# GpSimd's preparation products of a two-block layer kernel, queued behind the last gating product

## The chip, the core and the metric

The kernel runs on one core of a Trainium2 chip. The core has TensorE (PE, the matrix engine), VectorE (DVE), ScalarE (ACT), GpSimd (POOL) and SyncE (SP, which here only issues weight DMAs). Each engine works through its own queue in order, and an instruction that must wait for another engine holds up all behind it on its own engine. The metric is the time of one execution on the device, in microseconds (us).

## The reference, cut

Two layers follow each other on 256 tokens of width 1024. The stretch of interest is the feed-forward part at the end of the first layer, and what the second layer needs before it can start.

```python
def conv_glu_ffn(h, w_up, conv_w, w_down):          # D_FF = 2816 = 22 blocks of 128
    up = causal_dwconv(h @ w_up, conv_w)            # three taps along the positions
    gate, val = jnp.split(up, 2, axis=-1)
    return (jax.nn.silu(gate) * val) @ w_down

def s5_branch(u, a_re, a_im, log_dt, b_re, b_im, c_re, c_im, d, w_glu, b_glu):
    lam = lax.complex(a_re, a_im)
    a_bar = jnp.exp(lam * dt)
    b_bar = ((a_bar - 1.0) / lam)[..., None] * lax.complex(b_re, b_im)
    ...                                             # linear recurrence over the positions

def blockdiag(x, w):                                # w: (n_blocks, 4, 4)
    ...
gates = concat([q, k, v]) @ w_if + b_if             # q, k, v come out of blockdiag
```

The second layer's recurrence (`s5_branch`) is computed four positions at a time, so complex powers of `a_bar` times `b` and `c` are needed as matrices. Its gates are computed by folding the 4x4 blocks into `w_if`. Both depend on weights alone, so the kernel computes them while the first layer's feed-forward part runs. This is "the preparation".

## The kernel before, in words

**Weights.** All weight matrices arrive as units of eight 128x128 fp32 tiles (512 KB). For precision each unit is split in two fp32r parts: ScalarE rounds it to `wh` (L339), VectorE computes the remainder `wl` (L340). A product is then three matmuls (L405 to L407 in `mm3`): `wh` with the rounded activation, `wh` with its remainder, `wl` with the rounded activation. Four buffers each for `wh` and `wl` let the split run up to three units ahead of TensorE.

**The feed-forward loop.** `up(i)` for block i of 22 multiplies two units (48 matmuls into `u`), applies the three taps (ScalarE L1888, VectorE L1889 and L1890, for the gate half and the value half), then Silu on ScalarE (L1891), then the gating product of the two halves, L1892: on GpSimd for blocks 0 to 18, on VectorE for 19 to 21. "Product i" below is L1892 of block i. The result is split for the next matmuls: ScalarE rounds it to `ffnr` (L429 in `split`), VectorE computes the remainder (L430). `down(i - 2)` multiplies one unit (24 matmuls into `acc`, L1903 to L1905).

**The preparation.** `_prep` is a generator. Each time TensorE enters a new unit, `tick` lets it run one step, so its instructions are written in between the loop's. GpSimd does most of its work: eight complex products in `paced` (L564), each of four multiplies into the scratch `x1`, `x2` (tile ZZ, printed as s_3381) and two sums; three go to `bx` (tile BX, s_3382), one to `c0` (tile TT, s_3380), four to `cx` (tile CX, s_3379). With them go a small negation to `nc0` (L575) and a large one of 128x2048 elements (L583). Last come eight rounds of three block-diagonal expansions of 128x128 (`expand`, L492), each round followed by three small matmuls into `pf` (L639 to L641). The expansions of a round overwrite those of the round before, so they wait for its `pf`. TensorE also transposes `bx` (`pt`, L591, eight groups of four) and multiplies it by `c0` (`pk`, L599, four groups of 16); ScalarE copies the results out (L592, L602).

**What sets the order.** The tile framework keeps the dependencies and chooses for each engine an order by when it expects each instruction to be ready. So an instruction of `_prep` that depends on little can be put far ahead of its place in the program. `issue_after(ins)` adds, without a semaphore, the condition that what is written inside stands behind `ins` on `ins`'s engine.

Of the kernel before, what the change touches and what calls it, by code (L numbers as in the profile page):

```python
# [14 lines left out]
ALU = mybir.AluOpType  # L15
# [9 lines left out]
NFF = DFF // P  # L25
# [239 lines left out]
class _K:  # L265
    def __init__(self, ctx, tc, I):
        self.tc, self.nc, self.I = tc, tc.nc, I
        self.misc = ctx.enter_context(tc.tile_pool(name="misc", bufs=1))
        self.bigp = ctx.enter_context(tc.tile_pool(name="big", bufs=8))
        self.g8p = ctx.enter_context(tc.tile_pool(name="g8", bufs=3))  # L270
        self.wp = ctx.enter_context(tc.tile_pool(name="w", bufs=4))
        self.dram = ctx.enter_context(tc.tile_pool(name="dram", bufs=1, space=bass.MemoryType.DRAM))
        self.pl = ctx.enter_context(tc.tile_pool(name="pl", bufs=4, space=PSUM))
        self.banks = ctx.enter_context(ExitStack())
        self.pm = self.banks.enter_context(tc.tile_pool(name="pm", bufs=4, space=PSUM))
        self.src = [I["W"][u] for u in range(N_UNITS)] + [I["U"][i] for i in range(NE)] + [I["V"][i] for i in range(NE)]
        self.raw, self.units, self.done = [], {}, 0
        self.at = -1
        self.bg, self.credit, self.rate = [], 0.0, RATE
        self.splits, self.last = [], None  # L280
        self.n = 0

    def name(self, s):
# [64 lines left out]
    def behind(self, lag=0):  # L348

        s = ExitStack()  # L350
        for ins in (*self.splits[-1 - lag], self.last):
            if ins is not None:
                s.enter_context(self.tc.issue_after(ins))
        return s

    def step(self, gen, lag):
        if len(self.splits) <= lag:
# [110 lines left out]
def _prep(K, dump):  # L468

    nc, I, cols = K.nc, K.I, K.cols  # L470
    g = nc.gpsimd
    act, mm, tp = nc.scalar.activation, nc.tensor.matmul, nc.tensor.transpose
    tt, ts, stt = nc.vector.tensor_tensor, nc.vector.tensor_scalar, nc.vector.scalar_tensor_tensor
    EW, CX, TT, ZZ, BX = (K.big(f"s5{i}") for i in range(5))
    ew = EW.a(16, 2, P)
    cx = [CX.a(16, 4, 32) for _ in range(2)]
# [13 lines left out]
    def expand(w, e, dst):  # L490

        g.tensor_tensor(dst.rearrange("p (a b) -> p a b", b=4), _bc(w[:, 4 * e:4 * e + 4], 1, 32), _bc(msk, 2, 4), ALU.mult)  # L492
# [66 lines left out]
    def paced(dr, di, xr_, xi, yr, yi):  # L559

        ops = []
        cmul(dr, di, xr_, xi, yr, yi, x1, x2, lambda *z: ops.append(z))
        for n, z in enumerate(ops):
            g.tensor_tensor(*z)  # L564
            if n not in (0, 3):
                yield 0.1

# [4 lines left out]
    for t in (2, 1, 0):  # L572
        yield from paced(bx[0][:, :, t], bx[1][:, :, t], bx[0][:, :, t + 1], bx[1][:, :, t + 1], bar, bai)
    yield from paced(c0[0], c0[1], C[:, 0], C[:, 1], bc(kr), bc(ki))
    g.tensor_scalar(nc0, c0[1], -1.0, None, ALU.mult)  # L575

    def outputs():
        pr, pi_ = c0
        for t in range(4):
            qr, qi = cx[0][:, :, t], cx[1][:, :, t]  # L580
            yield from paced(qr, qi, pr, pi_, bar, bai)
            pr, pi_ = qr, qi
        g.tensor_scalar(cx[1], cx[1], -1.0, None, ALU.mult)  # L583

    def inputs():

# [45 lines left out]
    nc.vector.tensor_reduce(nqk, pr4.rearrange("p (m d) -> p m d", d=4), AX.X, ALU.add)  # L632

    for e in range(8):
        for i in range(3):
            expand(tr[i], e, ex[:, i])
        yield 0.3
        pf = K.ps("pf")
        mm(pf[:, 0:8], ex[:, 0], wif[:, e], start=True, stop=False)  # L639
        mm(pf[:, 0:8], ex[:, 1], wif[:, 8 + e], start=False, stop=True)  # L640
        mm(pf[:, 8:16], ex[:, 2], wif[:, 16 + e], start=True, stop=True)  # L641
        nc.scalar.copy(fold[:, :, e], pf[:, 0:16].rearrange("p (a b) -> p a b", a=2))
# [691 lines left out]
def trainium_kernel(ctx, tc, I, O, dump=None, stop=None):  # L1334
# [536 lines left out]
    def up(i):  # L1871
        nonlocal rs, nrm, prep
        u, raw = ua[i % 4], i < RAW
        if i == RAW:
            K.finish(nrm)
        ps = [K.ps("u"), K.ps("u")]
        for e in range(2):
            K.lin(f"up{i}", e * 8, 8, h0 if raw else hh, l0 if raw else hl, ps[e][:, :T1])
            if i == 0 and e == 1:
                rs = K.rstd()  # L1880
                nrm = K.start(K.normed(xr, COL["ffn_norm_g"], rs, hi1, lo1, T1))
                prep = K.start(_prep(K, dump))
            for f in (0, 1) if i == 0 and e else (e,) if i else ():
                v, n = ps[f][:, :T1], f * NFF + i
                if raw:
                    tt(uv[:, f], v, rs, ALU.mult)
                    v = uv[:, f]
                act(u[:, f], v, AF.Copy, scale=col("ffn_conv_w", 2 * 44 + n))  # L1888
                stt(u[:, f, 1:], v[:, :T1 - 1], col("ffn_conv_w", 44 + n), u[:, f, 1:], ALU.mult, ALU.add)  # L1889
                stt(u[:, f, 2:], v[:, :T1 - 2], col("ffn_conv_w", n), u[:, f, 2:], ALU.mult, ALU.add)  # L1890
        act(u[:, 0], u[:, 0], AF.Silu)  # L1891
        (nc.gpsimd.tensor_tensor if i < NFF - 3 else tt)(u[:, 0], u[:, 0], u[:, 1], ALU.mult)  # L1892
        if i > 0 and i <= NFF - 3:
            K.split(*uh[(i - 1) % 4], ua[(i - 1) % 4][:, 0])
        if i >= NFF - 3:
            K.split(*uh[i % 4], u[:, 0])
# [77 lines left out]
```

## Time and profile before

| | |
|---|---|
| median of 3 runs | 1595.97 us (1594.9 to 1597.15) |
| the profiled execution | 1592.86 us, of it a span of 1591.0 us |
| busy in the span | PE 1535.2 (96%), DVE 1146.4 (72%), ACT 832.5 (52%), POOL 237.4 us (15%) |
| chain that ended last | PE 84%, POOL 7% (L564 alone 4%), DVE 6%, ACT 1% |

The chain of work that ended last is read back from the last instruction to whatever released each. TensorE makes up most of it, as an engine that is busy 96% of the span would. GpSimd, busy 15% of the span, has 7% of the chain: that is its part of the time in which the end waited on it. Shares are means over the whole span; the rows further down cut out the stretch in question.

### The profile page before, as it was taken

The numbers are of one execution on the slowest core, as the hardware profiler recorded it, in microseconds if no ns is written. First come the engines' busy times: TensorE is split into PE (matmuls) and PEld (weight loads), VectorE is DVE, ScalarE is ACT, GpSimd is POOL, SyncE is SP. The second block draws the span as 40 slices with busy tenths as digits, with TensorE's granted clock in tenths as the row PEclk, the third lists the DMA queues.
The fourth block names the chain that finished last, engine by engine and source line by source line (L and its number), as shares of the span: only waits on it lengthen the run. The fifth ranks groups of instructions, "written<-read, shape, count | busy, mean of one in ns | idle before, by whom it ended". The sixth has DMA issues, their size and how long they took to land.

```text
span 1591.0 us, 29719 instructions
## 1 busy us (share of the span) xinstructions
PE 1535.2 (96%) x11661; PEld 1425.3 (90%) x11661; DVE 1146.4 (72%) x2164; ACT 832.5 (52%) x1439; POOL 237.4 (15%) x254
## 2 busy tenths in 40 slices
PE   7999999987599999999999999999999999999998
PEld 7999899987599997889999999999999888888886
DVE  7765467865477788668899888788999566566664
ACT  7654345744345556555554554544444555555554
POOL 2000000275613002000100431112222000000000
PEclk9999999998899999999999999999999999999999
DMA  7543245544255553245545555555545556556563
GB/s 258 160 136 119 80 133 173 193 146 136 91 174 163 171 166 111 93 134 167 190 159 183 177 158 186 161 161 170 159 160 165 185 194 196 191 195 192 193 197 107
DMA packets 80717, 257.94 MB, mean 162 GB/s; under 512 B 17345, under 2 KB 18881, under 8 KB 80322
## 3 DMA queue, kind: packets, MB, share of 16 engines
q1 hardware_dynamic: 69200, 247.32, 48.3%
q10 hardware_dynamic: 11378, 8.73, 1.9%
q8 instruction: 92, 1.51, 0.4%
q14 instruction: 47, 0.39, 0.1%
HBM read 253.23 MB, written 2.13 MB: 161 GB/s over the span
## 4 chain that ended last, share of the span: by engine, by line
PE 84%; POOL 7%; DVE 6%; ACT 1%; issue 1%; DMA 1%; SPq 0%; ACTq 0%; POOLq 0%; DVEq 0%
PE acc L1297 22%; PE U L405 7%; PE U L407 6%; PE U L406 6%; POOL s L564 4%; PE g L405 3%; PE g L406 3%; PE g L407 3%; DVE wl L340 2%; PE pG L1177 2%; PE u L405 2%; PE u L406 1%; PE u L407 1%; PE q L406 1%; PE q L405 1%; PE q L407 1%
## 5 line engine op out<-in xcount | busy, mean ns | idle before, releaser
L340 DVE TENSOR_TENSOR wl<-wr,wh 128x1024 fp32r<-128x1024 f32 (+1 forms) x469 | 587.4, 1255 | 196.0 <-ACT wh L339 193.1
L339 ACT CAST wh<-wr 128x1024 fp32r<-128x1024 f32 (+1 forms) x469 | 490.6, 1048 | 393.7 <-PE U L406 156.8
L1297 PE MATMUL acc<-wh,wring 128*128 128x512 f32 x1024 | 315.5, 389 | 0.0
L405 PE MATMUL U<-hh,wh 128*128 128x256 f32 x1024 | 292.5, 286 | 0.0
L407 PE MATMUL U<-hh,wl 128*128 128x256 f32 x1024 | 288.1, 281 | 1.5 <-DVE wl L340 1.4
L406 PE MATMUL U<-hl,wh 128*128 128x256 f32 x1024 | 288.3, 282 | 0.0
L1297 PEld LDWEIGHTS acc<-wh,wring 128*128 128x128 f32 x1024 | 192.2, 188 | 40.0
L1297 PE MATMUL acc<-wl,wring 128*128 128x512 f32 x512 | 199.2, 389 | 0.0
L407 PEld LDWEIGHTS U<-hh,wl 128*128 128x128 f32 x1024 | 193.9, 189 | 1.9 <-DVE wl L340 1.9
L405 PEld LDWEIGHTS U<-hh,wh 128*128 128x128 f32 x1024 | 193.4, 189 | 0.0
L406 PEld LDWEIGHTS U<-hl,wh 128*128 128x128 f32 x1024 | 192.5, 188 | 0.0
L1288 ACT ACTIVATE wring<-act 128x256 fp32r<-128x256 f32 x128 | 53.3, 418 | 152.2 <-PE acc L1297 148.7
L1297 PEld LDWEIGHTS acc<-wl,wring 128*128 128x128 f32 x512 | 96.1, 188 | 19.8
L405 PE MATMUL u<-hh,wh 128*128 128x256 f32 x320 | 92.9, 292 | 12.3 <-ACT wh L339 11.6
L1289 DVE SCALAR_TENSOR_TENSOR wring<-act,wring 128x256 fp32r<-128x256 f32 x128 | 54.6, 427 | 60.5 <-PE acc L1297 57.3
L407 PE MATMUL u<-hh,wl 128*128 128x256 f32 x320 | 92.0, 288 | 3.2 <-DVE wl L340 3.2
L406 PE MATMUL u<-hl,wh 128*128 128x256 f32 x320 | 91.4, 287 | 0.0
L1258 POOL TENSOR_TENSOR act<-act,ga 128x16 f32<-128x16 f32 (+31 forms) x77 | 56.5, 733 | 212.4 <-ACT ga L1257 192.3
L444 POOL TENSOR_TENSOR sq<-sq,sq 128x256 f32<-128x256 f32 x18 | 16.0, 888 | 415.4 <-ACT sq L440 415.1
L405 PEld LDWEIGHTS u<-hh,wh 128*128 128x128 f32 x320 | 62.3, 195 | 13.2 <-ACT wh L339 12.0
L405 PE MATMUL g<-hh,wh 128*128 128x256 f32 x256 | 73.8, 288 | 0.0
L406 PE MATMUL g<-hl,wh 128*128 128x256 f32 x256 | 72.0, 281 | 0.0
(643 smaller groups left out, 3411.6 us busy)
## 6 DMA issues: line engine op xcount, KB each, us to landing
wr<-in_W SPq DMA_DIRECT2D x211, 512.0 KB, 3.9
wr<-in_U SPq DMA_DIRECT2D x128, 512.0 KB, 3.9
wr<-in_V SPq DMA_DIRECT2D x128, 512.0 KB, 4.3
s<-in_s5p ACTq DMA_DIRECT2D x1, 1056.0 KB, 6.0
tkc<-in_keysT ACTq DMA_DIRECT2D x1, 1024.0 KB, 6.4
wsA<-in_cst ACTq DMA_DIRECT2D x1, 804.0 KB, 5.2
wsA<-in_rows ACTq DMA_DIRECT2D x1, 640.0 KB, 7.0
s<-s ACTq DMA_DIRECT2D x10, 64.0 KB, 3.0
```

The costliest lines, as they stand in the source:

```text
L339: a = nc.scalar.copy(hi[:, q], raw[:, q])
L340: b = nc.vector.tensor_tensor(lo[:, q], raw[:, q], hi[:, q].bitcast(F32), ALU.subtract)
L405: mm(out, wh, ah, start=first, stop=False)
L406: mm(out, wh, al, start=False, stop=False)
L407: self.last = mm(out, wl, ah, start=False, stop=last).ins
L444: self.nc.gpsimd.tensor_tensor(self.part[0], self.part[0], s, ALU.add)
L564: g.tensor_tensor(*z)
L1177: mm(o, ring[:, q % 2, e // 2, :, e % 2], ring[:, q % 2, 4 + 2 * w + e // 2, :, e % 2], start=w == 0, stop=w == 1)
L1258: g.tensor_tensor(d[:, :n], d[:, :n], a[:, :n], ALU.mult)
L1288: act(hi, w, AF.Copy, scale=1.0 / 16384)
L1289: stt(lo, w, 1.0 / 16384, hi.bitcast(F32), ALU.mult, ALU.subtract)
L1297: mm(acc[t][c], w[:, q], v[:, 4 * c:4 * c + 4].rearrange("p a b -> p (a b)"), start=False, stop=i == NE - 1 and len(vs) == 1, skip_group_c ...
```

## The change

`K.pace` holds the last gating product that was written for GpSimd. Every GpSimd operation of the preparation but the first memset is now written inside `K.paced()`, that is, behind that product on GpSimd. Once products move to VectorE (block 19) the condition ends. Line numbers of the changed kernel are higher: L569 is L564 of before, L581 is L575, L590 is L583, L496 is L492, L1900 is L1892, L647 to L649 are L639 to L641, and L1912 to L1914 are L1903 to L1905.

```diff
-        self.splits, self.last = [], None
+        self.splits, self.last, self.pace = [], None, None
...
+    def paced(self):
+
+        return ExitStack() if self.pace is None else self.tc.issue_after(self.pace)
...
         for n, z in enumerate(ops):
-            g.tensor_tensor(*z)
+            with K.paced():
+                g.tensor_tensor(*z)
             if n not in (0, 3):
                 yield 0.1
...
-    g.tensor_scalar(nc0, c0[1], -1.0, None, ALU.mult)
+    with K.paced():
+        g.tensor_scalar(nc0, c0[1], -1.0, None, ALU.mult)
...
-        g.tensor_scalar(cx[1], cx[1], -1.0, None, ALU.mult)
+        with K.paced():
+            g.tensor_scalar(cx[1], cx[1], -1.0, None, ALU.mult)
...
-        for i in range(3):
-            expand(tr[i], e, ex[:, i])
+        with K.paced():
+            for i in range(3):
+                expand(tr[i], e, ex[:, i])
...
-        (nc.gpsimd.tensor_tensor if i < NFF - 3 else tt)(u[:, 0], u[:, 0], u[:, 1], ALU.mult)
+        prod = (nc.gpsimd.tensor_tensor if i < NFF - 3 else tt)(u[:, 0], u[:, 0], u[:, 1], ALU.mult)
+        K.pace = prod.ins if i < NFF - 3 else None
```

GpSimd's queue in the middle of the loop, before: the end of the sixteen preparation operations that stand ahead of product 5, then products 5 to 8 in one row, then the preparation again.

```order
L564 TENSOR_TENSOR s_3380<-s_3381 128x512
L564 TENSOR_TENSOR s_3381<-s_3381,s_3380 128x512 x2
L564 TENSOR_TENSOR s_3380<-s_3381 128x512
L575 TENSOR_SCALAR s_3381<-s_3380 128x512
L564 TENSOR_TENSOR s_3381<-s_3380 128x512 x2
L1892 TENSOR_TENSOR ffn_2985<-ffn_2985 128x256 x4
L564 TENSOR_TENSOR s_3379<-s_3381 128x16x32
```

The same operations of GpSimd's queue now; the three products in these rows are 8, 9 and 10.

```order
L569 TENSOR_TENSOR s_3380<-s_3381 128x512
L1900 TENSOR_TENSOR ffn_2985<-ffn_2985 128x256
L569 TENSOR_TENSOR s_3381<-s_3381,s_3380 128x512 x2
L569 TENSOR_TENSOR s_3380<-s_3381 128x512
L581 TENSOR_SCALAR s_3381<-s_3380 128x512
L569 TENSOR_TENSOR s_3381<-s_3380 128x512 x2
L1900 TENSOR_TENSOR ffn_2985<-ffn_2985 128x256
L569 TENSOR_TENSOR s_3379<-s_3381 128x16x32
L569 TENSOR_TENSOR s_3381<-s_3380 128x512 x2
L569 TENSOR_TENSOR s_3379<-s_3381 128x16x32
L1900 TENSOR_TENSOR ffn_2985<-ffn_2985 128x256
```

Each product has moved between preparation operations that used to run as one block. The last operation for `bx`, the matrix that `pt` reads, now follows product 7 directly.

GpSimd's queue at the end of the loop, before: the large negation, then products 10 to 15 with only a memset between them, then products 16, 17 and 18 with expansions between (the first round of expansions stands far ahead, before product 0).

```order
L583 TENSOR_SCALAR s_3379<-s_3379 128x2048
L1892 TENSOR_TENSOR ffn_2985<-ffn_2985 128x256 x3
L671 MEMSET ml_5925 128x8x3
L1892 TENSOR_TENSOR ffn_2985<-ffn_2985 128x256 x3
L492 TENSOR_TENSOR ml_3383<-ml_3383 128x128 x9
L1892 TENSOR_TENSOR ffn_2985<-ffn_2985 128x256
L492 TENSOR_TENSOR ml_3383<-ml_3383 128x128 x8
```

The same place now, from product 14 on.

```order
L1900 TENSOR_TENSOR ffn_2985<-ffn_2985 128x256
L590 TENSOR_SCALAR s_3379<-s_3379 128x2048
L1900 TENSOR_TENSOR ffn_2985<-ffn_2985 128x256
L496 TENSOR_TENSOR ml_3383<-ml_3383 128x128 x6
L1900 TENSOR_TENSOR ffn_2985<-ffn_2985 128x256
L496 TENSOR_TENSOR ml_3383<-ml_3383 128x128 x9
L1900 TENSOR_TENSOR ffn_2985<-ffn_2985 128x256
L496 TENSOR_TENSOR ml_3383<-ml_3383 128x128 x12
L1900 TENSOR_TENSOR ffn_2985<-ffn_2985 128x256
```

The large negation stands between products 14 and 15, the first two rounds of expansions behind product 15, three rounds behind 16 and the rest behind 17.

TensorE's queue at the third `pf` (pf_5273), before: it stands between the end of one `down` (acc) and the next `up` (u).

```order
L1903 MATMUL acc_3287<-ffnr_2986,wh_5144 128x256
L1904 MATMUL acc_3287<-ffnr_2986,wh_5144 128x256
L1905 MATMUL acc_3287<-ffnr_2986,wl_5145 128x256
L639 MATMUL pf_5273<-ml_3383 128x8
L640 MATMUL pf_5273<-ml_3383 128x8
L641 MATMUL pf_5273<-ml_3383 128x8
L405 MATMUL u_5265<-hh_3282,wh_5182 128x256
```

And now:

```order
L1914 MATMUL acc_3287<-ffnr_2986,wl_5145 128x256
L1912 MATMUL acc_3284<-ffnr_2986,wh_5267 128x256
L1913 MATMUL acc_3284<-ffnr_2986,wh_5267 128x256
L1914 MATMUL acc_3284<-ffnr_2986,wl_5268 128x256
L1912 MATMUL acc_3284<-ffnr_2986,wh_5267 128x256
L1913 MATMUL acc_3284<-ffnr_2986,wh_5267 128x256
L1914 MATMUL acc_3284<-ffnr_2986,wl_5268 128x256
L1912 MATMUL acc_3285<-ffnr_2986,wh_5267 128x256
L1913 MATMUL acc_3285<-ffnr_2986,wh_5267 128x256
L647 MATMUL pf_5273<-ml_3383 128x8
L648 MATMUL pf_5273<-ml_3383 128x8
L409 MATMUL u_5265<-hh_3282,wh_5182 128x256
```

Eight matmuls of the following `down` (unit 5267) have been taken in front of this `pf`. In the same way 31 stand in front of the sixth; the places of the other six `pf`, of `pt` and of `pk` in TensorE's queue are unchanged.

## Rows read from the trace of the kernel before

**Rows 1.** Busy tenths of PE and POOL in 40 equal slices, from the page.

```profile
PE   7999999987599999999999999999999999999998
POOL 2000000275613002000100431112222000000000
```

**Rows 2.** Windows: us, busy us (count) of PE, PEld, DVE, ACT, POOL; clock, DMA, GB/s.

```profile
340.00:360.00 20.00, 14.63 (x99) 13.93 (x97) 7.21 (x8) 4.39 (x7) 19.37 (x16) 0.83 0.31 103
...
400.00:420.00 20.00, 11.00 (x91) 10.38 (x89) 7.97 (x8) 5.84 (x10) 19.21 (x16) 0.92 0.26 79
...
440.00:460.00 20.00, 20.00 (x173) 20.00 (x172) 9.74 (x26) 6.35 (x11) 2.49 (x3) 1.00 0.53 135
```

**Rows 3.** Waits, 340 to 440 us: total us, times, longest us.

```profile
ACT ffnr L429 <- POOL ffn L1892: 56.6, 8, 16.6
```

**Rows 4.** Timeline of ACT: start, us, operation, in brackets idle before and releaser.

```profile
348.32 0.42 ACT L1891 ACTIVATE ffn<-ffn 128x256 f32<-128x256 f32 x1 [1.43 <-DVE ffn L1890]
...
366.13 0.40 ACT L429 CAST ffnr<-ffn 128x256 fp32r<-128x256 f32 x1 [16.45 <-POOL ffn L1892]
...
400.21 0.41 ACT L429 CAST ffnr<-ffn 128x256 fp32r<-128x256 f32 x1 [5.41 <-POOL ffn L1892]
...
472.12 0.42 ACT L1891 ACTIVATE ffn<-ffn 128x256 f32<-128x256 f32 x1
```

**Rows 5.** Timeline of PE.

```profile
340.13 0.28 PE L405 MATMUL u<-hh,wh 128*128 128x256 f32 x1
...
367.53 0.58 PE L405 MATMUL u<-hh,wh 128*128 128x256 f32 x1 [9.46 <-ACT wh L339]
...
387.49 0.60 PE L591 MATMUL pt<-eye,s 128*128 128x128 f32 x4
387.85 0.36 PE L405 MATMUL u<-hh,wh 128*128 128x256 f32 x1
...
402.19 0.63 PE L591 MATMUL pt<-eye,s 128*128 128x128 f32 x4 [1.47 <-ACT s L592]
...
427.41 1.11 PE L591 MATMUL pt<-eye,s 128*128 128x128 f32 x4 [14.43 <-ACT s L592]
...
432.21 1.87 PE L599 MATMUL pk<-s,s 128*128 128x32 f32 x16
433.91 0.36 PE L405 MATMUL u<-hh,wh 128*128 128x256 f32 x1
...
447.80 0.36 PE L405 MATMUL u<-hh,wh 128*128 128x256 f32 x1
...
456.43 0.28 PE L405 MATMUL u<-hh,wh 128*128 128x256 f32 x1
...
464.99 0.28 PE L405 MATMUL u<-hh,wh 128*128 128x256 f32 x1
...
476.40 0.28 PE L639 MATMUL pf<-ml 128*128 128x8 f32 x2
```

**Rows 6.** Timeline of POOL.

```profile
335.75 3.90 POOL L564 TENSOR_TENSOR s<-s,s 128x512 f32<-128x512 f32 x2
...
354.94 2.06 POOL L564 TENSOR_TENSOR s<-s,s 128x512 f32<-128x512 f32 x2
357.08 1.28 POOL L564 TENSOR_TENSOR s<-s 128x512 f32<-128x512 f32 x1
...
419.44 5.36 POOL L583 TENSOR_SCALAR s<-s 128x2048 f32<-128x2048 f32 x1
...
474.88 0.76 POOL L1892 TENSOR_TENSOR ffn<-ffn 128x256 f32<-128x256 f32 x1 [6.95 <-DVE s L554]
...
480.25 1.44 POOL L492 TENSOR_TENSOR ml<-ml 128x128 f32<-128x128 f32 x3 [2.04 <-PE pf L639]
```

**Rows 7.** Timeline of DVE: the remainder of a weight unit, three in a row and one alone.

```profile
332.85 5.89 DVE L340 TENSOR_TENSOR wl<-wr,wh 128x1024 fp32r<-128x1024 f32 x3
...
374.84 1.23 DVE L340 TENSOR_TENSOR wl<-wr,wh 128x1024 fp32r<-128x1024 f32 x1 [0.52 <-ACT wh L339]
```

## The prediction

> **What bounds the kernel now.** The span is TensorE's: PE is busy in nine tenths or more of nearly every one of the 40 slices [rows 1], and the exceptions worth a look are slices 8 to 10 (318 to 438 us), where its digits fall to 8, 7 and 5 while POOL's, elsewhere near nothing, rise to 7, 5 and 6. So I cut that stretch into 20 us windows [rows 2]. In an undisturbed window (440 to 460) PE starts 173 matmuls at a granted clock of 1.00. From 340 to 360 it starts 99, with 14.63 us busy and 0.83 granted; from 400 to 420 it starts 91, with 11.00 us busy.
>
> Who holds it up: the longest wait between 340 and 440 us is that of ScalarE's L429 (the rounding of a gated block to fp32r) for POOL's L1892, the gating product, 56.6 us in 8 waits [rows 3]. ScalarE is in order, and behind L429 stand the weight roundings (L339) that PE needs. The order of POOL shows the reason: before product 4 (the L1892 of block 4) it holds 10 operations of the preparation, before product 5 sixteen, before products 9 and 10 eight and fifteen, and none before products 6, 7 and 8. Silu of block 5 is done at 348.7 us, and ScalarE gets past L429 only at 366.13, after 16.45 us of idling [rows 4]. PE outlives the first part of such a block, since roundings run up to three units ahead, and then stands still: 9.46 us before 367.53 and 14.43 us before 427.41 [rows 5].
>
> What that costs in all I take from PE's own order. An undisturbed iteration of the feed-forward loop (48 matmuls of `up`, 24 of `down`) takes 464.99 - 456.43 = 8.56 us. Between the starts of two blocks at 340.13 and 447.80 lie seven iterations, and in them eight groups of transposes `pt` (387.85 - 387.49 = 0.36 us each) and four groups of `pk` (433.91 - 432.21 = 1.70 us each) [rows 5]. Undisturbed that is 7 x 8.56 + 8 x 0.36 + 4 x 1.70 = 59.9 + 2.9 + 6.8 = 69.6 us; it took 107.67. **Lost: 38.1 us**, partly idle, partly matmuls after each halt at a lower granted clock [rows 2].
>
> **The change part by part.** No operation is added or taken away, and ScalarE, VectorE and SP keep their orders but for two or three neighbours. POOL's order is what moves.
>
> *The clumps go.* Between two products now stand 3, 5, 4, 5, 4, 6, 4, 5, 4, 5, 4 preparation operations, then one 128x2048 negation, then 6, 9 and 12 block-diagonal expansions. The question is whether POOL gets through each group within an iteration. Undisturbed, two multiplies take 2.06 us and the third operation 1.28, with gaps 3.49 per three [rows 6]; a product takes 0.76. Four operations are then 4.85 us, five 5.6, and six with the small negation 7.1. But POOL slows when VectorE works: the pair at 335.75 takes 3.90 instead of 2.06 us [rows 6], in the time in which VectorE's L340 takes 5.89 us for three where one alone takes 1.23 [rows 7]. Two of these L340 lie beside the pair, so 2 x 1.13 us (1.23 less the 0.1 by which neighbours overlap, an estimate) cost POOL 1.84: a share of 0.8. An iteration has three L340 and one L430 of a quarter their size, 3 x 1.13 + 0.3 = 3.7 us, or 3.0 us of delay for POOL. Its iteration is therefore 4.85 + 0.76 + 3.0 = 8.6 us with four operations, 9.4 with five, 10.9 with six. Against that PE gives 8.56 us for blocks 5 to 8, 8.9 and 9.6 for 9 to 11 (the `pt`), and 11 to 12 for 12 and 13 (the `pk`). Adding up the differences, the product comes late by 0.8, 0.8, 1.6, 1.6 us at blocks 5 to 8, 3.6 at 9, 2.6 at 10, 2.4 at 11, and has caught up by 13.
>
> *What such lateness costs.* Before 400.21, L429 of block 9 kept ScalarE idle for 5.41 us [rows 4], and PE then stood for 1.47 us, before 402.19, at a `pt` [rows 5]; outside the `pt` stretch it outlived 8.4 us (from 366.13 - 16.45 to 367.53 - 9.46) [rows 4, 5]. So lateness up to 3.6 us costs between 0 and 1.5 us in all. I take 0.7.
>
> *Preparation products that now come later.* The transposes `pt` need all 18 products of `bx`, of which the last now runs right behind product 7. That is about 2 + 0.8 + 1.4 + 1.6 = 5.8 us after block 7's last matmul; the first `pt` stands two `down` groups, one `up` and half of another behind it, 2 x 2.85 + 5.7 + 2.85 = 14.3 us. Nothing lost, 8 us to spare; if that cover went, each us late would be a us of PE. `pk` has more. The negation (5.36 us [rows 6]) moves from behind the last product of the second clump to between products 14 and 15; its reader is hundreds of matmuls away.
>
> *The expansions and `pf`.* Here the change makes a new wait on PE's path. The first expansion used to stand ahead of product 0 in POOL's order; now it stands behind product 15, and the first `pf`, in the middle of block 16, waits for it. In times of the profile before: Silu of block 15 ends at 472.54, product 15 ran at 474.88 to 475.64 (late, beside a run of small VectorE operations), three expansions take 1.44, so 477.1 against the 476.40 at which PE comes to `pf` [rows 4, 5, 6]. With the negation in front, product 15 may be some 2 us later still. PE stops for 0 to 3 us; I take 1.2. `pf` 2 and `pf` 5 stand behind products 16 and 17; the order puts 8 and 31 matmuls of the next `down` ahead of them, which covers all but about 0.9 and 0.2 us. The other five follow their own expansions as before. Together 2.3 us.
>
> **Sum.** The profiled execution took 1592.86 us (span 1591.0): 1592.86 - 38.1 + 0.7 + 2.3 = 1557.8. The median of the runs shown is 3.1 us above the profiled one, so in its terms **1561 us**. What is late next is nothing: after 447 us PE is busy throughout [rows 2], and all behind the loop shifts by the same amount.
>
> **The rivals.** *A. POOL becomes the pace.* The share of 0.8 rests on one pair. If VectorE's two-input operations cost POOL their full time, blocks 5 to 15 need, for 46 operations, a large negation, eleven products and VectorE's part, 52.3 + 6.9 + 8.4 + 11 x 3.7 + 4 = 112 us (4 for the small operations of blocks 13 to 15), against the 11 x 8.56 + 9.7 = 103.9 that PE gives. With 0.8 it is 103.4, just even: that is why this rival is real. At the full price POOL runs 8 us over, and with up to 5 us for `pf` the result is 1558 + 13 = 1571, or 1574 in terms of the median. [...] I give it 0.13.
>
> *B. Slower than before: halts in most iterations, each with a slow restart.* If product after product is late by more than PE can outlive, PE halts once an iteration, and after a halt it runs at a lower granted clock. The window from 340 to 360 shows the price: 74 matmuls missing, 74 x 0.119 = 8.8 us, of which 5.4 idle and 3.4 at lower clock [rows 2]; without the start of the next halt (about 1.9 us idle) one halt costs 6.9. It decides from six halts (38.1 / 6.9 = 5.5); with eight, the time is 1558 + 8 x 6.9 + 3 = 1616 us. For it: POOL has no slack from block 5 to 11. Against it: that needs a period of 10.6 us where my sums give 8.6 to 9.4, and PE's halt of 1.47 us at 402.19 lies in a window that was still granted 0.92, with the long halt at its end [rows 2, 5]. Chance 0.03.
>
> *C. The stall only moves.* If the expansions, or ScalarE's weight roundings for another reason, hold PE for as long as POOL did, the gain is within 3 us of nothing: 1596. The same wait list has nothing else above 25 us that PE inherits; 0.02.
>
> **How the numbers follow.** Forecast 1561 with 0.82, A 1574 with 0.13, B 1616 with 0.03, C 1596 with 0.02. The bounds of the forecast's own terms give 1558 (no residual) to 1564 (1.5 + 3 + 1.1 of it); the runs of the kernel before spread over 2.3 us, and its halts before 340 us, which I did not count, may shrink as well. So the range goes down to 1554, and up to 1575, to take in A. A measurement of this kernel can tell about 0.2%, 3 us: faster 0.95, within it 0.02, slower 0.03.
>
> **What would show it.** In the profile of the changed kernel: POOL's digits spread evenly over slices 8 to 11 instead of the 7, 5, 6; the wait of L429 for the product falls from 56.6 us to under 20; PE 172 or so matmuls in every 20 us window from 340 on, granted 1.00; `up` of block 13 starts near 410 us instead of 447.80; short PE waits at `pf` for POOL, 1 to 3 us in all. Right in the main but wrong in size: PE waits of 1 us or more for L339 or `pt` in each of blocks 7 to 11 (rival A), with L340 at about 2 us. Wrong: L429 waits of 10 us again, or a granted clock of 0.5 between 340 and 420 us.

## The result, and the profile after

The changed kernel takes **1572.69 us** (median of 4 runs, 1571.1 to 1575.74), the kernel before 1595.43 us (4 runs, 1593.64 to 1597.15). The ratio is 0.986, with a 95% interval of 0.9841 to 0.9879: faster by 23 us, 11.7 us less than the 34.4 us (1595.43 - 1561) that were forecast. The profiled execution took 1575.74 us, of it a span of 1573.9; a second profile of the same kernel, taken with the experiments, has a span of 1568.8.

In the rows from here on L433 and L434 are L429 and L430 of before, L409 to L411 are L405 to L407, L1896 to L1899 are L1888 to L1891, L598 and L599 are L591 and L592, and L556 to L561 are small VectorE operations of the preparation on 128x16 elements. In the rows of an experiment a line of the changed kernel can be up to four off.

The busy tenths of PE and POOL, from the page of the changed kernel, against [rows 1]:

```profile
PE   7999999999989999999999999999999999999998
POOL 1000000269742011000101421112222000000000
```

The 8, 7 and 5 of PE in slices 8 to 10 (counted from 0) are gone, and PE has a new 8, in slice 11. POOL's 7, 5, 6, 1, 3 of slices 8 to 12 have become 6, 9, 7, 4, 2: not as even as forecast, and in slice 9 nearly without a pause. Windows of the changed kernel (us, busy us (count) of PE, PEld, DVE, ACT, POOL; clock, DMA, GB/s), three of them those of [rows 2]:

```profile
340.00:360.00 20.00, 20.00 (x170) 20.00 (x169) 17.59 (x19) 9.81 (x16) 19.46 (x13) 1.00 0.66 211
400.00:420.00 20.00, 20.00 (x175) 20.00 (x174) 16.36 (x17) 8.44 (x14) 14.66 (x11) 1.00 0.45 147
440.00:460.00 20.00, 14.86 (x98) 14.40 (x97) 17.62 (x56) 6.53 (x12) 8.52 (x8) 0.83 0.49 160
460.00:480.00 20.00, 18.08 (x134) 17.35 (x133) 10.02 (x15) 6.63 (x15) 8.96 (x17) 0.91 0.38 119
```

The first two windows went from 99 and 91 matmuls to 170 and 175 at a granted clock of 1.00. The third, undisturbed before, now has 98 and a granted clock of 0.83. The waits between 340 and 440 us (total us, times, longest), against [rows 3], show that the product's wait has shrunk to a third, from 56.6 us:

```profile
ACT ffn L1899 <- DVE ffn L1898: 23.4, 9, 6.5
ACT ffnr L433 <- POOL ffn L1900: 17.7, 9, 3.6
```

PE's waits between 416 and 490 us are almost all at `pf`, for the expansions:

```profile
PE pf L647 <- POOL ml L496: 6.1, 2, 5.1
PE acc L1914 <- DVE wl L340: 1.1, 1, 1.1
PE pf L649 <- POOL ml L496: 0.7, 1, 0.7
```

To see where the time went I cut PE's timeline at four starts: the first matmul of block 6, of block 13, of block 16, and the first of the transposes `pm` behind block 18. These are the three stretches of the changed kernel (same columns as above):

```profile
342.79:416.17 73.38, 71.07 (x603) 70.41 (x601) 60.21 (x63) 35.03 (x58) 65.11 (x43) 1.00 0.51 165
416.17:443.29 27.12, 26.01 (x218) 25.80 (x218) 23.50 (x34) 13.58 (x21) 20.72 (x14) 1.00 0.62 161
443.29:489.18 45.89, 38.84 (x280) 37.63 (x279) 29.12 (x78) 16.35 (x35) 17.82 (x31) 0.89 0.40 128
```

The kernel before takes 107.67, 25.75 and 30.87 us for them, the last two with PE never idle:

```profile
447.80:473.55 25.75, 25.75 (x218) 25.75 (x218) 19.28 (x50) 12.67 (x20) 3.42 (x3) 1.00 0.65 182
473.55:504.42 30.87, 30.87 (x266) 30.87 (x265) 24.70 (x61) 14.83 (x32) 15.09 (x27) 1.00 0.51 164
```

So 34.3 us are won in blocks 6 to 12, and 1.4 and 15.0 us are lost behind them. In the last stretch the count says 280 against 266: 14 more matmuls stand ahead of `pm` there, work of 1.7 us (at 8.56 / 72 = 0.119 us each) that is missing behind it. The real loss is 45.89 - 30.87 - 1.7 = **13.3 us**: 45.89 - 38.84 = 7.05 us in which PE stands still, and 38.84 - 30.87 - 1.7 = 6.3 us in which the matmuls take longer. Most of the 6.3 us is a lower granted clock: 0.89 over 45.89 us is 5.0 us less than full. Not all of it is, since e1 below has 1.0 us of it at a granted clock of 1.00. This split is made for each kernel below; each ratio is to runs of the kernel before that were made beside it:

| kernel | median us | ratio to before, 95% | idle in blocks 16 to 18 | slower matmuls there | sum |
|---|---|---|---|---|---|
| changed | 1572.69 | 0.9841 to 0.9879 | 7.05 | 6.3 | 13.3 |
| e11, the changed kernel again | 1572.81 | 0.9841 to 0.9874 | 7.08 | 3.7 | 10.8 |
| e1, expansions free | 1562.91 | 0.9762 to 0.9813 | 1.95 | 1.0 | 2.9 |
| e2, expansions alone paced | 1602.99 | 1.0025 to 1.0059 | 2.87 | 4.8 | 7.7 |
| e3, negation in four | 1570.14 | 0.9801 to 0.9857 | 4.84 | 6.0 | 10.8 |
| e4, e1 and e3 | **1560.29** | 0.975 to 0.9801 | 0.02 | 0.4 | 0.4 |
| e5, first round free | 1578.91 | 0.9864 to 0.991 | 7.01 | 6.6 | 13.6 |
| e10, e5 again | 1577.11 | 0.9864 to 0.9908 | 6.46 | 7.2 | 13.7 |
| e6, one product back | 1566.5 | 0.9795 to 0.9836 | 2.21 | 3.7 | 5.9 |
| e7, eight more multiplies | 1579.15 | 0.9868 to 0.9927 | 7.15 | 6.1 | 13.2 |
| e8, negation on ScalarE | 1570.9 | 0.982 to 0.9865 | 4.42 | 5.9 | 10.3 |
| e9, e1 and e8 | 1562.36 | 0.9764 to 0.9825 | 0 | 0 | 0 |

### The profile page after: what moved, and what is told of

It reads as the page before. It is cut to its first block, busy times and chain, and to the rows that moved or that the text cites. A ratio compares the mean times of both kernels' runs of the same rounds, so it can differ in the third digit from the quotient of the medians.

```text
span 1573.9 us, 29717 instructions
## 1 busy us (share of the span) xinstructions
PE 1537.4 (98%) x11661; PEld 1427.6 (91%) x11661; DVE 1163.2 (74%) x2164; ACT 832.0 (53%) x1439; POOL 249.5 (16%) x254
## 4 chain that ended last, share of the span: by engine, by line
PE 83%; DVE 8%; POOL 4%; ACT 2%; issue 1%; DMA 1%; SPq 0%; ACTq 0%; DVEq 0%; POOLq 0%
PE acc L1305 22%; PE U L409 7%; PE U L411 7%; PE U L410 7%; DVE wl L340 4%; PE g L409 3%; PE g L410 3%; PE g L411 3%; PE pG L1185 2%; POOL s L569 2%; PE u L409 1%; PE u L410 1%; PE u L411 1%; PE q L410 1%; PE q L409 1%
## 5 line engine op out<-in xcount | busy, mean ns | idle before, releaser
L340 DVE TENSOR_TENSOR wl<-wr,wh 128x1024 fp32r<-128x1024 f32 (+1 forms) x469 | 596.3, 1274 | 200.1 <-ACT wh L339 196.7
L409 PE MATMUL U<-hh,wh 128*128 128x256 f32 x1024 | 292.9, 286 | 0.0
L411 PE MATMUL U<-hh,wl 128*128 128x256 f32 x1024 | 288.4, 282 | 1.5 <-DVE wl L340 1.4
L411 PEld LDWEIGHTS U<-hh,wl 128*128 128x128 f32 x1024 | 194.3, 190 | 1.9 <-DVE wl L340 1.9
L409 PEld LDWEIGHTS U<-hh,wh 128*128 128x128 f32 x1024 | 193.7, 189 | 0.0
L409 PE MATMUL u<-hh,wh 128*128 128x256 f32 x320 | 92.5, 291 | 1.4 <-DVE ffn L1898 1.2
L411 PE MATMUL u<-hh,wl 128*128 128x256 f32 x320 | 91.7, 288 | 0.8 <-DVE wl L340 0.8
L409 PE MATMUL g<-hh,wh 128*128 128x256 f32 x256 | 73.9, 289 | 0.0
L411 PE MATMUL g<-hh,wl 128*128 128x256 f32 x256 | 72.0, 281 | 0.0
```

The costliest lines, as they stand in the source:

```text
L340: b = nc.vector.tensor_tensor(lo[:, q], raw[:, q], hi[:, q].bitcast(F32), ALU.subtract)
L409: mm(out, wh, ah, start=first, stop=False)
L411: self.last = mm(out, wl, ah, start=False, stop=last).ins
```

## The experiments

All edits are to the changed kernel. **The theory after the result:** the pacing of the block products gives most of what was forecast, and the pacing of the expansions takes a part of it back, because their rounds now wait for gating products and `pf` on TensorE waits for them. The rivals: that the long negation alone makes product 15 late and so the halts; that the residue is POOL as the pace, since it and VectorE slow each other (3.90 us instead of 2.06 for a pair of multiplies, [rows 6]; the expectations call this rival "port"); that the loss is the granted clock's own, with no cause in the order.

### Expansions free or paced, negation whole or split

e1 leaves the expansions where the scheduler puts them:

```diff
-        with K.paced():
-            for i in range(3):
-                expand(tr[i], e, ex[:, i])
+        for i in range(3):
+            expand(tr[i], e, ex[:, i])
```

> The changed kernel, but the expansions (L496) are again written without the condition; the complex products and both negations keep it. Theory (new waits): the shortfall against the forecast sits where TensorE waits for the expansions, 15.0 us between the starts of blocks 16 and 19 in the trace after, so without the condition on them the time is 1572.7 - 15.0 = 1558 us (1556 to 1561), and no pf waits for GpSimd. Rival (port): VectorE and GpSimd hinder each other all through the loop and that is what is missing; then this kernel stays at 1568 us or more.

It took 1562.91 us, 9.8 less than the changed kernel and 1.9 above the theory's range. One wait at `pf` is left, at the second, where none was expected: its round stands behind product 15, which is as late as in the changed kernel. The second row is its stretch of blocks 16 to 18.

```profile
449.54 0.39 PE L646 MATMUL pf<-ml 128*128 128x8 f32 x2 [1.68 <-POOL ml L496]
```

```profile
441.17:474.99 33.82, 31.87 (x267) 31.21 (x266) 29.26 (x77) 14.85 (x33) 17.17 (x28) 1.00 0.57 175
```

e2 is the other half: the multiplies and both negations lose their condition, the expansions keep it.

```diff
-            with K.paced():
-                g.tensor_tensor(*z)
+            g.tensor_tensor(*z)
...
-    with K.paced():
-        g.tensor_scalar(nc0, c0[1], -1.0, None, ALU.mult)
+    g.tensor_scalar(nc0, c0[1], -1.0, None, ALU.mult)
...
-        with K.paced():
-            g.tensor_scalar(cx[1], cx[1], -1.0, None, ALU.mult)
+        g.tensor_scalar(cx[1], cx[1], -1.0, None, ALU.mult)
```

> The kernel before, and only the expansions are queued behind the last product; the complex products and negations stand in clumps as before. Theory (new waits): the 38 us of the clumps stay, and pf gets its new waits on top. How large: if the large negation in front of product 15 made the first wait long, it is short here (the negation is done 50 us earlier), about 1 us, and with pf 3 and pf 6 some 4 us: 1599 us (1597 to 1602). If the negation has no part in it, the whole 15 us comes on top: 1610 us. Rival (port): the expansions do not matter, 1595 us.

It is slower than before, by 0.25 to 0.59%, and at 1602.99 us 1 us above the theory's range. The clumps are back (108.07 us for blocks 6 to 12), and pacing the expansions costs 7.7 us in blocks 16 to 18 although the negation is out of the way. The idle part is 2.87 us, two halts of about 1 us and three of a quarter, against 7.05; the rest comes after the halts, as in this window of 5 us, with PE busy throughout:

```profile
490.00:495.00 5.00, 5.00 (x31) 5.00 (x31) 0.00 (x0) 0.85 (x2) 1.14 (x4) 0.66 0.36 108
```

e3 splits the large negation into four and queues each behind the products of the loop:

```diff
+            if t:
+                with K.paced():
+                    g.tensor_scalar(cx[1][:, :, t - 1], cx[1][:, :, t - 1], -1.0, None, ALU.mult)
...
-            g.tensor_scalar(cx[1], cx[1], -1.0, None, ALU.mult)
+            g.tensor_scalar(cx[1][:, :, 3], cx[1][:, :, 3], -1.0, None, ALU.mult)
```

> The changed kernel with the condition on everything, but the negation of 128x2048 elements is cut into four of 128x512 elements, two of them one and two products earlier and two at its old place. If the one long operation keeps VectorE from its two-input operations (one of 16 elements took 3.60 us beside it) and so makes Silu of block 15 and the first pf late, the halt of 5.09 us falls to 2 to 3 us, and with the restart 3 to 5 us are saved: 1568 to 1570 us. If the negation only adds its own 5 to 6 us of GpSimd time, 1571 to 1573 us, since two of four pieces still stand there.

1570.14 us: the first halt shrinks to 2.78 us, and little else follows.

```profile
445.53 0.50 PE L650 MATMUL pf<-ml 128*128 128x8 f32 x2 [2.78 <-POOL ml L496]
```

e4 has both edits.

> Both edits: expansions without the condition, and the negation in four pieces. Theory (new waits): as with the free expansions alone, 1556 to 1559 us, since without a pf wait the late Silu of block 15 is outlived. If the negation costs TensorE something of its own through late weight remainders, this kernel is 2 us or more below the one with free expansions and a whole negation. Rival (port): 1568 us or more.

1560.29 us, 1.3 above the theory's range and the lowest median of all, though its interval overlaps with those of e1 and e9. There is no wait at `pf` in blocks 16 to 18:

```profile
439.25:470.51 31.26, 31.24 (x266) 31.06 (x265) 26.72 (x69) 14.97 (x33) 16.36 (x27) 1.00 0.58 183
```

The two edits add up: -9.8 for the expansions, -2.6 for the negation, -12.4 together. The theory holds, and the first rival has only the smaller part. e4 stands at 1560.3, where 1561 was forecast: about what the change would have given without the wait at `pf`.

### Only the first round free: a miss

If the price were the first halt of 5.09 us, taking its round out of the condition would be enough.

```diff
-        with K.paced():
+        with K.paced() if e else ExitStack():
```

> The changed kernel, with the condition taken from the first round of expansions alone; rounds 2 to 8 keep it. Theory (several new waits, each with a slow restart): the first pf has no wait (5.1 us of halt and 3.3 us until the second pf are saved), the second waits for round 2, which now stands behind product 15 (about 2 us, as with all expansions free), and the third and sixth keep their 1 to 2 us of halt and their restarts. From block 16 to 19 about 40 us instead of 45.9 and 33.8 with all free: 1566 to 1568 us. Rival (only the first pf matters, the others are covered by the matmuls put ahead of them): 1562 to 1564 us.

It took 1578.91 us, *more* than the changed kernel. The first `pf` doesn't wait, but PE's timeline shows what was late next:

```profile
449.01 0.39 PE L647 MATMUL pf<-ml 128*128 128x8 f32 x2 [1.64 <-POOL ml L496]
449.65 0.39 PE L648 MATMUL pf<-ml 128*128 128x8 f32 x2 [0.25 <-POOL ml L496]
455.49 0.39 PE L1914 MATMUL acc<-ffnr,wl 128*128 128x256 f32 x1 [1.85 <-DVE wl L340]
458.55 0.39 PE L647 MATMUL pf<-ml 128*128 128x8 f32 x2 [2.09 <-POOL ml L496]
474.43 0.39 PE L647 MATMUL pf<-ml 128*128 128x8 f32 x2 [1.03 <-POOL ml L496]
```

The second round waits for product 15 and the third for product 16, which can't start before TensorE has finished block 16. TensorE comes to these `pf` earlier now and waits there instead, and for 1.85 us at a weight remainder (L340): 7.01 us idle against 7.05. The halt had been hiding the ones behind it. Behind `pm`, where nothing was changed, e5's profile takes 5.8 us more than the changed kernel's (1090.5 against 1084.7). These lie in the second layer and are the subject of e10 below.

### One product of distance

e6 keeps the rounds in a fixed order, but behind the product *before* the last one:

```diff
-        with K.paced():
+        with ExitStack() if K.pace is None or K.pace0 is None else K.tc.issue_after(K.pace0):
...
-        K.pace = prod.ins if i < NFF - 3 else None
+        K.pace0, K.pace = K.pace, prod.ins if i < NFF - 3 else None
```

> The expansions are queued behind the gating product before the last one, everything else as in the changed kernel. So round 1 follows the large negation, ahead of product 15, and rounds 2 to 4 follow product 15. Theory: what costs in blocks 16 to 18 is that each round's pf needs a product whose input TensorE has only just finished; one product of distance breaks that. Then the stretch from the start of block 16 to the transposes after block 18 loses under 4 us (as with free expansions, 2.95), and the median is 1560 to 1566 us. Rival: the condition itself, with its other order on TensorE, costs even where the rounds come early: 10 us or more lost in that stretch and 1570 us or more.

1566.5 us, half a us above the theory's range: 5.9 us are lost and not under 4.

```profile
441.37:478.15 36.78, 34.57 (x266) 34.05 (x265) 29.91 (x77) 15.02 (x33) 18.81 (x31) 0.91 0.51 161
```

The halts are those of e1, at the second `pf` only (1.96 and 0.25 us); what exceeds is 3.7 us of slower matmuls against 1.0, at a granted clock of 0.91 against 1.00. So of the 13.3 and 10.8 us that the changed kernel loses in its two profiles 5.9 are left when a round is no longer tied to the product of the block that has only just left TensorE. Two things stay open: whether the 3.0 us that e6 loses beyond e1 belong to the condition or are chance, and what TensorE's other order costs by itself, since e6 has the order of before again (266 matmuls ahead of `pm`, and 24 of `down` ahead of the third `pf`).

### Where the negation's part comes from

e8 gives the large negation to ScalarE, which does it in 1.92 us; e9 does so with free expansions.

```diff
-        with K.paced():
-            g.tensor_scalar(cx[1], cx[1], -1.0, None, ALU.mult)
+        act(cx[1], cx[1], AF.Copy, scale=-1.0)
```

> The changed kernel, with the negation of 128x2048 elements on ScalarE instead of GpSimd. Theory (the long GpSimd operation keeps VectorE off, and with it Silu of block 15 and product 15): the first pf halts for about 1 us instead of 5.1, and pf 3 and pf 6 as before; block 16 to 19 takes about 40 us, block 13 to 16 25.8: 1565 to 1568 us, more than the 2.6 us that cutting it in four saved. Rival (the negation matters only by its length in GpSimd's queue, and ScalarE's 2 us come in its place): 1569 to 1571 us.

> Expansions without the condition and the negation on ScalarE. Theory: no new wait is left, and block 13 to 19 takes what it took before the change (25.8 + 30.9 us); what remains against the kernel before is the 34 us saved in blocks 6 to 13: 1559 to 1561 us, like the kernel with free expansions and the negation in four pieces. If ScalarE's 2 us delay the weight roundings, 1562 us or more.

Both times came out in the rival's range: 1570.9 and 1562.36 us. The theory's mechanism is there all the same. The VectorE operation of 16 elements that takes 3.60 us beside the negation in the changed kernel (shown further down) takes 0.70 us in e8, and product 15 starts 3.09 us after block 16 on TensorE (444.25 against 441.16) instead of 6.01 (449.30 against 443.29):

```profile
434.95 0.70 DVE L556 TENSOR_TENSOR s<-s 128x16 f32<-128x16 f32 x1
444.25 0.74 POOL L1899 TENSOR_TENSOR ffn<-ffn 128x256 f32<-128x256 f32 x1 [8.62 <-DVE s L561]
```

The first `pf` waits twice, for 1.26 and 1.06 us, instead of 5.09. What the theory had too small is the rest: 5.9 us are still lost in slower matmuls, at a granted 0.88, where the changed kernel's two profiles lose 6.3 and 3.7. With the expansions free the negation costs nothing in blocks 16 to 18 (e9: 30.87 us, the time of before); blocks 13 to 15 take 27.12 us there, as in the changed kernel, and not 25.8.

### Is POOL the pace in blocks 5 to 13?

e7 writes the first multiply of each of the eight complex products twice, eight more operations for POOL:

```diff
             with K.paced():
+                if n == 0:
+                    g.tensor_tensor(*z)
                 g.tensor_tensor(*z)
```

> The changed kernel, and the first multiply of each of the eight complex products is written twice, so GpSimd has eight more operations of 1.1 to 1.5 us between blocks 4 and 13 and computes the same. It measures how much GpSimd time the loop still covers. Theory (the groups just fit, products are up to 3.6 us late): lateness grows by about 1 us an iteration and TensorE loses part of it, 4 to 8 us: 1577 to 1581 us. Rival (port: GpSimd already is the pace of these blocks): all of it, 10 to 14 us: 1583 to 1587 us. If there were much room left, 1573 us.

1579.15 us, as the theory had it. Blocks 6 to 12 take 77.51 us instead of 73.38, POOL is busy for 72.68 of them instead of 65.11. Of 7.6 us of added work 4.1 reach TensorE, 2.1 of them as idle time (4.40 against 2.31 us) and 2.0 as slower matmuls at a granted 0.98.

```profile
342.21:419.72 77.51, 73.11 (x602) 72.05 (x601) 59.84 (x63) 35.03 (x58) 72.68 (x49) 0.98 0.49 156
```

POOL has a little room left in the changed kernel, and no more, which agrees with the sums that made it "just even".

### The same programs again

e10 and e11 are e5 and the changed kernel once more, without an edit, beside e6 on one chip.

> The kernel with only the first round of expansions free, once more. Its first profile lost 13.6 us in blocks 16 to 18, as the changed kernel does (13.3), and 5.8 us more in the second layer, where the same halt of 1.41 us was followed by 33 instead of 58 matmuls in 8 us. Theory: the granted clock after that halt belongs to the program and its timing, so it shows again: 1576 to 1580 us, and 190 or so matmuls in the 32 us around that halt, against 216 in the changed kernel. Rival: it falls by chance from execution to execution; then this profile may show 216, and the median is 1571 to 1575 us.

> The changed kernel once more, beside the two others on the same chip. Both theories: 1571 to 1576 us. With a clock that belongs to the program, 216 matmuls in the 32 us around the 1.41 us halt of the second layer, as in its first profile; with one that falls by chance, 190 as likely as 216.

1577.11 and 1572.81 us, so the difference of e5 is no accident. In the second layer PE has one halt of 1.41 us, of the same kind and place in all kernels (`pN`, waiting for VectorE), besides shorter ones. These are the 8 us behind it, first in the changed kernel, then in e5:

```profile
689.18:697.18 8.00, 8.00 (x58) 6.96 (x56) 7.78 (x22) 7.15 (x20) 0.00 (x0) 1.00 0.61 199
```

```profile
686.82:694.82 8.00, 8.00 (x33) 7.02 (x32) 4.88 (x14) 3.58 (x12) 0.00 (x0) 0.53 0.62 204
```

58 matmuls at a granted clock of 1.00, 33 at 0.53. In the 32 us around it the changed kernel starts 216 and 217 matmuls (first and second profile), e5 192, e10 197. The first of these and the last:

```profile
669.18:701.18 32.00, 30.59 (x216) 26.55 (x216) 21.91 (x55) 18.91 (x47) 0.00 (x0) 1.00 0.44 132
666.76:698.76 32.00, 30.59 (x197) 26.31 (x196) 19.37 (x46) 17.67 (x40) 0.00 (x0) 0.89 0.39 111
```

In two profiles each, the drop stays with the program, if not to the last matmul. It makes up 4.8 of e5's 5.8 us. The other 0.9 us are a drop from 527.0 to 530.5 us, in which matmuls start 0.23 us apart where the changed kernel's start 0.13 apart; e10 has it too, and no halt of PE stands just before it. e2's profile has the drop behind the 1.41 us as well (192 matmuls, 5.8 us more behind `pm`), which may be why that execution is 5.4 us above e2's median. What in the timing decides whether the clock falls there was not tried, and stays open. For the split inside blocks 16 to 18 chance does have a part. The changed kernel has the same halts in both profiles (7.05 and 7.08 us idle), and 6.3 against 3.7 us of slower matmuls, at a granted 0.89 and 0.92:

```profile
440.92:484.22 43.30, 36.22 (x280) 34.99 (x279) 29.18 (x78) 16.39 (x35) 17.88 (x31) 0.92 0.43 136
```

## Why the prediction was right or wrong, point by point

**The bound and the clumps: right.** POOL's clumps were what held ScalarE, and through it TensorE. With them gone the stretch from block 6 to block 13 falls from 107.67 to 73.38 us, 34.3 us of the 38.1 that were called lost. `up` of block 13 starts at 416.17 instead of the "near 410": 73.38 - 69.6 is 3.8 us of the difference, and 2.66 us more come from this execution's start of block 6 (342.79 against 340.13). In the second profile block 6 starts at 340.40, so nearly all of these 2.66 us belong to the execution and not to the change.

**How late the products come: right in sum, not block by block.** The list above has 17.7 us in 9 waits of L433 for the product, under the 20 that were named. For products 5 to 11 they are 2.4, 2.6, 3.6, 2.3, 3.2, 0.5 and 0.5 us, 15.0 together, where the sums had a lateness of 0.8, 0.8, 1.6, 1.6, 3.6, 2.6 and 2.4, 13.4 together. That the longest wait equals the largest lateness of the sums is chance: it is behind product 7, not 9. The share of 0.8 was not measured again; e7 agrees with a POOL that just keeps up. The two longest on ScalarE's timeline, for products 7 and 9:

```profile
366.54 0.41 ACT L433 CAST ffnr<-ffn 128x256 fp32r<-128x256 f32 x1 [3.56 <-POOL ffn L1900]
384.64 0.41 ACT L433 CAST ffnr<-ffn 128x256 fp32r<-128x256 f32 x1 [3.24 <-POOL ffn L1900]
```

**What it costs: 2.3 us of idling, not 0.7.** PE stands three times in these blocks, twice at `up` (0.67 and 0.53 us, for the taps of an earlier block, L1898) and once at a `pt` (1.12 us); the first and the last are shown. The other 1.5 us of the 3.8 are an error of the yardstick: PE's busy time at a granted clock of 1.00 is 71.07 us, where 69.6 had been put together from gaps of the profile before. So only 36.6 us had been lost there.

```profile
379.16 0.39 PE L409 MATMUL u<-hh,wh 128*128 128x256 f32 x1 [0.67 <-DVE ffn L1898]
386.62 0.63 PE L598 MATMUL pt<-eye,s 128*128 128x128 f32 x4 [1.12 <-ACT s L599]
```

**Blocks 13 to 15: 1.4 us that no step had.** 1.11 us of it is one wait of `acc` for a weight remainder (L340). The two L340 around it take 2.05 and 1.92 us, where one alone took 1.23 [rows 7], and POOL multiplies beside them; that this makes the wait was not tried.

**The expansions and `pf`: the step that failed.** "Together 2.3 us" measured 13.3 and, in the second profile, 10.8. The mechanism was named, and two things were mis-sized.

*First, product 15.* It "may be some 2 us later still"; it is 4.7 us later (6.01 us after block 16's start against 1.33 before, from 474.88 and 473.55). VectorE, POOL and ScalarE of the changed kernel show the way:

```profile
438.78 3.60 DVE L556 TENSOR_TENSOR s<-s 128x16 f32<-128x16 f32 x1
448.68 0.47 DVE L1898 SCALAR_TENSOR_TENSOR ffn<-u,cols,ffn 128x254 f32<-128x254 f32 x1
```

```profile
437.74 6.34 POOL L590 TENSOR_SCALAR s<-s 128x2048 f32<-128x2048 f32 x1
449.30 0.73 POOL L1900 TENSOR_TENSOR ffn<-ffn 128x256 f32<-128x256 f32 x1 [5.21 <-DVE s L558]
450.00 3.77 POOL L496 TENSOR_TENSOR ml<-ml 128x128 f32<-128x128 f32 x6
```

```profile
446.54 0.42 ACT L1899 ACTIVATE ffn<-ffn 128x256 f32<-128x256 f32 x1 [3.46 <-DVE s L558]
```

Beside the negation an operation of 16 elements keeps VectorE for 3.60 us (the same operation takes 3.60 in e6 and 3.61 in e11, with the negation whole on GpSimd as well; 0.70 in e8 and e9, with it on ScalarE; 0.74 in the kernel before, without it there), and the taps of block 15 queue up behind it. Silu comes at 446.54, the last tap of the value half ends at 449.15, and the product follows at 449.30. The wait that the prediction read in [rows 6] as POOL being "late beside a run of small VectorE operations" is this one: the product doesn't run slowly, it waits for a tap that stands among those operations on VectorE. So whatever holds VectorE there holds `pf`. Without the negation on POOL (e8) product 15 is 1.8 us later than before, so 2.9 of the 4.7 us are the negation's; where the 1.8 come from stays open. PE then waits 5.09 us at the first `pf`, where 1.2 was taken and 3 was the upper end:

```profile
451.62 0.60 PE L647 MATMUL pf<-ml 128*128 128x8 f32 x2 [5.09 <-POOL ml L496]
464.72 0.39 PE L649 MATMUL pf<-ml 128*128 128x8 f32 x2 [0.73 <-POOL ml L496]
478.33 0.39 PE L647 MATMUL pf<-ml 128*128 128x8 f32 x2 [1.04 <-POOL ml L496]
```

The waits behind products 16 and 17 were to be 0.9 and 0.2 us and are 0.73 and 1.04: the first was well sized, the second five times too small. They add up with the wait at the first `pf` to 6.9 of the 7.05 us.

*Second, the clock.* Each halt was priced at its idle time. Rival B had the price of a slow restart in its sum; the `pf` term had not. Windows of 5 us after the halts, with PE busy throughout:

```profile
455.00:460.00 5.00, 5.00 (x32) 5.00 (x31) 2.79 (x13) 1.58 (x3) 0.00 (x0) 0.67 0.36 105
465.00:470.00 5.00, 5.00 (x31) 5.00 (x32) 0.00 (x0) 0.81 (x2) 1.27 (x4) 0.66 0.35 108
480.00:485.00 5.00, 5.00 (x45) 5.00 (x44) 1.56 (x2) 1.59 (x4) 1.36 (x4) 1.00 0.19 68
```

32 and 31 matmuls instead of 45, at 0.67 and 0.66. Both windows hold two levels: us by us the granted clock is 0.50 up to 458 and 1.00 from 459 on in the first, 0.50 from 466 to 468 and 1.00 from 469 on in the second. This narrower window shows the lower level alone:

```profile
453.00:456.00 3.00, 3.00 (x15) 3.00 (x15) 2.89 (x11) 0.17 (x1) 0.74 (x2) 0.50 0.29 109
```

After the third halt the clock stays at 1.00. So beside 7.1 us of standing still, slower matmuls cost 6.3 us in one profile of this program and 3.7 us in the other, most of it by the clock. What decides between 6.3 and 3.7 was not shown: the two profiles stand still for 7.05 and 7.08 us, at a granted 0.89 and 0.92 over the stretch. Stretches at a granted 0.50 are there elsewhere too: the first profile has two within its first 50 us, from 18.0 to 21.3 and from 46.0 to 48.0. For the halt in the second layer the drop stays with the program (216 and 217 matmuls against 192 and 197).

**The sum.** The forecast for the profiled execution was 1557.8. Add 3.1 us (3.8 instead of 0.7 in blocks 6 to 12), 1.4 (blocks 13 to 15), 11.0 (13.3 instead of 2.3 at `pf`) and the 2.7 us by which this execution came later to block 6: 1576.0, against a measured 1575.74. In the median the `pf` term is nearer to the second profile's 10.8.

**The range.** The measured 1572.69 us lies within 1554 to 1575 only because the range was stretched to take in rival A; the bounds of the forecast's own terms ended at 1564. A did not happen, as the next paragraph shows. So that the range held is luck.

**The rivals.** A gave a time that fits, 1574, but not for its reason. POOL didn't become the pace in blocks 5 to 11: PE starts 170 and 175 matmuls per 20 us there, at 1.00, and the 8 us that A expected lost along them are 2.3. e7 shows how near it was. No run shows the full price that A's 112 us take: in the 100.5 us of blocks 6 to 15 of the changed kernel (73.38 and 27.12) POOL is busy for 85.8 (65.11 and 20.72). That VectorE and GpSimd slow each other ([rows 6, 7]) shows itself in a place where the prediction hadn't looked: in the 3.60 us of a 16-element operation beside the negation, against 0.70 with the negation on ScalarE (e8). It does not last as long as the negation: by the profile, whose spans on POOL are rough, the negation runs from 437.74 to 444.08 us, but the 16-element operation ends at 442.38, and an L340 takes 1.21 us from 442.39 on, as one alone does (1.23 in [rows 7]). B's halts came three times and not eight, and in other blocks. C, a stall that only moves, is a third of the truth: some 12 of 34 us came back, nearly all at `pf`. It was weighed with 0.02 by the waits on the list of before; the wait that came is one that the change itself makes.

## What to carry to other kernels

Whoever ties background work to the loop should tie it to an output of an iteration earlier, or not at all where nothing asks for it, and not to the newest: what waits for the newest waits for the matmuls that TensorE has just left, and hands the wait back to TensorE (e6 and e1 against the changed kernel, 6 and 10 us). A halt of TensorE on the path costs what it stands still and can cost slower matmuls on top: in the two profiles of the changed kernel half as much to nearly as much again, in e6 3.7 us behind 2.2, in e1 1.0 behind 2.0. Taking away the first of several halts can give nothing (e5), since the next ones were behind it. Pacing the block products and leaving the expansions free, with the long negation cut in four, has the lowest median: 1560.29 us, 0.975 to 0.9801 of the time before.

## What the runs showed of the hardware

- A VectorE operation of 128x16 elements took 3.60 us beside a GpSimd operation of 128x2048 (6.34 us there, 5.36 in [rows 6]), and 0.70 us with that operation on ScalarE (e8); the next two of the same size took 0.16 us each in the changed kernel, at 442.31 and 443.52 us, before that operation's end at 444.08.
- ScalarE negates 128x2048 elements in 1.92 us (e8), GpSimd in 5.36 (the kernel before) and 6.34 (the changed kernel).
- A halt of 0.73 us at `pf` was followed by a granted 0.66, one of 1.04 us by 1.00, and one and the same halt of 1.41 us in the second layer by 1.00 in one program and 0.53 in another. A halt of 1.68 us at the second `pf` was followed by a granted 1.00 over the stretch in e1; behind one of 1.96 us at the same place in e6 the matmuls start 0.21 us apart up to 456.78, and 0.12 apart from 457.95 on. The length of a halt alone doesn't tell what it costs.
